# A hybrid recurrence and mixture-of-experts layer on one core: the first block's token list summed while experts are chosen

## The chip, the cores and the metric

The kernel runs on one core of a Trainium2 chip. The metric is the device time of one execution, in microseconds (us); lower is better.

## The reference, cut to what matters

One layer with 2048 tokens of 1024 channels: a mixer (a gated linear recurrence and a spatial gate behind one input projection, then one output projection with a residual), and then a mixture of experts with a residual, and a last RMSNorm. All is float32. The change touches the experts:

```
logits_g = h @ w_group + b_group          # 4 groups
logits_e = h @ w_router + b_router        # 32 experts, 8 in a group
g_sel    = argmax(logits_g)
top-2 of the 8 experts inside g_sel, weights = softmax
...
order    = argsort(expert)                # tokens sorted by expert,
padded   = ceil(counts / 128) * 128       # each expert's list filled up to blocks of 128
def expert_block(xb, e):                  # for each block
    return (silu(xb @ w_gate[e]) * (xb @ w_up[e])) @ w_down[e]
```

An expert's three matrices are 1024 x 512, 1024 x 512 and 512 x 1024: 2 MB each.

## The kernel before

The mixer fills the first 1120 us. Its last stage, `output_projection`, goes through 16 tiles of 128 tokens, from tile 15 down to tile 0. TensorE multiplies; VectorE adds the residual; a router's product gives the logits. `choose` takes the tiles in groups (12 to 15, 8 to 11, 4 to 7, 2 and 3, last 0 and 1): it finds each token's two experts as one-hot rows (`pick`), counts tokens by expert (`sums`), and gives each token its place in its expert's list: a block (`blk`) and a row in it, as a one-hot row of 128 (`at`). The tile's normalized rows `h` are stored to DRAM (`h_d`).

Then `routing`, a chain of small steps: counts of all tokens (`total`), blocks by expert (`ni`, `nb`), an order of experts (`key`, `ahead`), each expert's first block (`start`), and for four groups of four tiles a matrix `v`, whose product with `at` (64 matmul records on TensorE) sums up every block's token list. `index` is that table: column j has the 128 token numbers of block j.

`experts` works through the blocks. `load` brings an expert's matrices in six DMAs of 1 MB from SyncE's queue into `st` (two sets, for even and odd blocks). `high` and `low` split a staged matrix into two float32r parts (`wh` on ScalarE, `wl` on VectorE), so that a product is three matmuls of float32r: high by high, high by low, low by high. `fetch` is an indirect DMA of GpSimd's queue that gathers a block's 128 rows from `h_d` into `xg`. `turn_rows` transposes them on TensorE and splits them into `xh`, `xl`. `collect` weights the result and adds it to the rows of `acc_d`.

A scheduler sets the order of each engine's instructions, from a cost model and from priorities, except where `pin` keeps the order of the code. Each engine issues in its own order and waits there for what its next instruction needs; this holds for the DMAs that it issues too. Tiles come from pools of SBUF; a pool opened later takes the place of a closed one, and a tile in it waits until the last reader of what lay there is done. Here pool `lg` (logits and all of `routing`'s tables) is closed before pool `sp` opens at the same side. PSUM has eight banks in the first part; the tag `t2` is one of them, so a tile of `t2` waits for the reader of the one before.

Of the kernel before, what the change touches and what calls it, by code (L numbers as in the profile page):

```python
# [14 lines left out]
F32 = mybir.dt.float32  # L15
F32R = mybir.dt.float32r
# [9 lines left out]
P = 128  # L26
# [34 lines left out]
class Mixer:  # L61
# [617 lines left out]
    def output_projection(self, op, lg):  # L679
        nc, I = self.nc, self.I  # L680
        wh, wl = zip(*self.wo)
        with self.tc.tile_pool(name="os", bufs=2, reuse_waits="tile") as os_:
# [6 lines left out]
            def project(t, y, between, before):  # L689
# [29 lines left out]
                def normed(parts=(0, 1)):  # L719
                    for s in [fs[f] for f in parts]:  # L720
                        nc.vector.scalar_tensor_tensor(h[:, s], x[:, s], st[:, 2:3], rows["a2"][:, s], op0=ALU.mult, op1=ALU.mult)
                        nc.vector.tensor_add(h[:, s], h[:, s], rows["b2"][:, s])
                    if 1 in parts:

                        (nc.sync if t else nc.gpsimd).dma_start(self.h_d[t * P : (t + 1) * P], h)

                return x, st[:, 2:3], normed

# [50 lines left out]
            columns(done[0], done[1], 1)  # L779
            logits(0, *done[1:])  # L780
            chosen = self.choose(op, 0, 2, os_)
            with self.tc.issue_after(next(chosen)):
                normed((1,))
            next(chosen, None)
            self.routing(lg, os_)


    def routing_start(self, rt):
# [3 lines left out]
        def new(shape, name, dt=F32, **iota):  # L792
            x = rt.tile([P] + list(shape), dt, name=name)
            if iota:
                nc.gpsimd.iota(x, allow_small_or_imprecise_dtypes=True, **iota)
            return x
# [11 lines left out]
            "w": new([2, NT], "w"),  # L808
            "blk": new([2, NT], "blk"),
            "at": new([2, NT, P], "at"),  # L810
        }
        nc.gpsimd.memset(R["before"], 1.0)
        nc.gpsimd.affine_select(out=R["before"], in_=R["before"], compare_op=ALU.is_gt, fill=0.0, base=0, pattern=[[1, P]], channel_multiplier=-1)
        nc.vector.memset(R["sums"][:, NT], 0.0)
# [23 lines left out]
    def choose(self, L, t0, tn, tp):  # L838
# [5 lines left out]
        def new(shape, name, dt=F32):  # L844
            return tp.tile([P] + list(shape), dt, name=name, bufs=1)
# [47 lines left out]
        nc.vector.scalar_tensor_tensor(rw, R["blk"][:, :, ts], -float(P), place, op0=ALU.mult, op1=ALU.add)  # L893
        nc.vector.tensor_tensor(R["at"][:, :, ts], R["rows"].unsqueeze(1).unsqueeze(1).to_broadcast([P, 2, tn, P]), rw.unsqueeze(3).to_broadcast([P, 2, tn, P]), op=ALU.is_equal)

        e = new([tn, NG], "e")
        nc.vector.tensor_tensor(e, lg, bc(gm, [tn, NG], 2), op=ALU.subtract)
        nc.scalar.activation(e, e, AF.Exp)
# [6 lines left out]
        nc.vector.reciprocal(w1, den)  # L905
        nc.vector.tensor_mul(w2, w2, w1)

    def routing(self, rt, rv):


        nc, R, S = self.nc, self.R, self.tab
        new, row = R["new"], R["row"]

        total = self.psum("t1")
        nc.tensor.matmul(total[:, :NE], self.ones, R["sums"][:, 0], start=True, stop=True)
        nc.tensor.matmul(total[:, NE : NE + 1], R["sums"][:, : P // NE].rearrange("p t e -> p (t e)"), self.ones[:, :1], start=True, stop=True)
        ni = new([NE + 1], "ni", I32)
        nc.vector.tensor_scalar_add(ni, total[:, : NE + 1], float(P - 1))
        nc.vector.tensor_scalar(ni, ni, 7, None, op0=ALU.arith_shift_right)
# [61 lines left out]
    def experts(self, mp, sp, pp):  # L981
# [3 lines left out]

        xg = [mp.tile([P, D], F32, name=f"xg{n}") for n in range(2)]

        for x in xg:
            nc.gpsimd.memset(x, 0.0)
        acts = [mp.tile([P, 512], F32, name=f"a{n}") for n in range(2)]  # L990


        small = mp.tile([P, 96], F32, name="small")
        rows = [[sp.tile([P, KD, P], F32R, name=f"x{x}{n}") for x in "hl"] for n in range(2)]
        sp.tile([P, 64], F32, name="pad")
        parts = [[[sp.tile([P, 2, D], F32R, name=f"w{x}{s}{n}") for n in range(2)] for s in range(2)] for x in "hl"]
        g2 = self.row(sp, "g2")


        stage = [[[sp.tile([P, 2, D], F32, name=f"st{s}{part}{n}") for n in range(2)] for part in range(3)] for s in range(2)]  # L1000
# [51 lines left out]

        def fetch(j):
            if j <= MAXB:
                rows = bass.IndirectOffsetOnAxis(ap=S["index"][:, j : j + 1], axis=0)
                dma = nc.gpsimd.indirect_dma_start(xg[j % 2], None, self.h_d[:, :], rows, bounds_check=T - 1, oob_is_err=False)  # L1056
                self.got = dma.ins

# [40 lines left out]
        def sums():  # L1099
            return pp.tile([P, 2, 512], F32, name="sums", bufs=1)  # L1100

        def steps(js, end=None, whole=None):

            for j in js:
                a = acts[j % 2]
                if end is None:
                    fetch(j + 2)
                pg = bank()  # L1110
                product(j, 0, range(4), pg)
                if j:
                    high(j - 1, 2, 0)
                    high(j - 1, 2, 1)
                    low(j - 1, 2, 0, end)
                    act = turn_act(acts[(j - 1) % 2])
                    low(j - 1, 2, 1, end)
                if end is not None:
                    yield
                product(j, 0, range(4, KD), pg)  # L1120
                if j:
                    high(j, 1, 0)
                    low(j, 1, 0, end)
                    pin(nc.scalar.activation(a, pg, AF.Silu))
                high(j, 1, 1)
                low(j, 1, 1, end)
                if end is not None:
                    yield
                if not j:
                    pin(nc.scalar.activation(a, pg, AF.Silu))  # L1130
                    turn_rows(j + 1)
                else:
                    pd = sums()
                    down(j - 1, act, range(2), pd)
                    if end is None:
                        turn_rows(j + 1)
                    down(j - 1, act, range(2, 4), pd)
                    collect(j - 1, pd)
                    if j + 1 == end:
                        px = turn_rows(j + 1)  # L1140
                pu = bank()
                product(j, 1, range(KD), pu)
                if j != end:
                    high(j + 1, 0, 0)
                    low(j + 1, 0, 0, end)
                    high(j + 1, 0, 1)
                    if whole is not None:
                        pin(nc.scalar.activation(whole, px, AF.Copy))
                    pin(nc.vector.tensor_mul(a, a, pu))
                    low(j + 1, 0, 1, end)  # L1150
                else:
                    for n in range(2):
                        high(j, 2, n)
                        low(j, 2, n, end)
                    pin(nc.vector.tensor_mul(a, a, pu))
                if j + 1 == end:
                    yield
# [180 lines left out]

        for part in range(3):
            load(0, part)  # L1340
        place[0, 0] = 0
        for n in range(2):
            split(parts[0][0][n], parts[1][0][n], stage[0][0][n])
        fetch(0)
        high(0, 1, 0)
        low(0, 1, 0)
        turn_rows(0)
        for part in range(3):
            load(1, part)
        load(2, 0)  # L1350
        fetch(1)
        run(steps(range(MINB - 2)))
        with ExitStack() as behind:
            last = {i.engine: i for i in nc.cur_bb.bb.instructions}
            for engine in (SP, mybir.EngineType.PE, mybir.EngineType.Activation, mybir.EngineType.DVE, mybir.EngineType.Pool):
# [210 lines left out]
def layer(tc, ctx, I, out=None):  # L1566
# [26 lines left out]
    with tc.tile_pool(name="pp", bufs=1, space=PSUM) as pp:  # L1593
        M.pp = pp
        hp = ExitStack()
        with pool("ms", bufs=1) as ms:
# [6 lines left out]
        tab = ctx.enter_context(pool("tab", bufs=1))  # L1603
        M.tab = {
            "index": tab.tile([P, 64], I32, name="index"), "weight": tab.tile([P, 64], F32, name="weight"),
            "expert": tab.tile([1, NJ], I32, name="expert"), "fresh": tab.tile([1, NJ], I32, name="fresh"), "count": tab.tile([1, 16], I32, name="count")[:, :1],
        }
        with pool("lg", bufs=1, side="right") as lg:
            L = lg.tile([P, NT, NG + NE], F32, name="L")
            M.output_projection(L, lg)  # L1610
# [28 lines left out]
```

## Time and profile before

| | us |
|---|---|
| median of 3 runs | 2057.06 |
| lowest, highest | 2056.17, 2058.30 |
| the profiled execution, its own time | 2056.24 |
| its span, first to last instruction | 2054.5 |

A profile names instructions by line, engine, operation and tile. Busy time says how long an engine worked; the chain of waits says, followed back from the last instruction, which work or wait ended last at each moment. Times in the trace are counted from the span's start. The stretch that the change touches lies between 1120 and 1190 us: the end of the output projection, the routing, and the first block.

### The profile page before, as it was taken

How to read it: one execution, taken by the hardware profiler on the slowest of the kernel's cores; microseconds unless marked ns; L12 is line 12 of the kernel's file. 1: busy time of each engine (PE TensorE's matmuls, PEld its weight loads, DVE VectorE, ACT ScalarE, POOL GpSimd, SP SyncE). 2: the span in 40 equal slices, each digit the busy share in tenths (PEclk: the TensorE clock that was granted, in tenths of full speed). 3: DMA queues.
4: the chain of work that ended last, by engine and by line, in shares of the span. 5: the costliest groups of instructions: out<-in, count | busy, mean ns of one | idle time of the engine just before them, and what ended most of it. 6: DMA issues, size and time to landing. Idle time of an engine off the chain costs nothing.

```text
span 2054.5 us, 27982 instructions
## 1 busy us (share of the span) xinstructions
PE 1978.5 (96%) x9833; PEld 1630.2 (79%) x9833; DVE 1535.9 (75%) x2135; ACT 1113.1 (54%) x1265; POOL 310.1 (15%) x242
## 2 busy tenths in 40 slices
PE   7999999999999999989999599999999999999994
PEld 3787887888888888878888488888888888888881
DVE  6653337566666666646776799999999999999995
ACT  3664321334434344354542277777777777777773
POOL 1000001000000000110000122222222222232323
PEclk9999999999999999999999699999999999999997
DMA  7433749333333333486553888898887559888857
GB/s 277 148 116 102 249 149 320 125 104 104 119 105 116 101 104 114 156 273 223 187 197 118 326 298 262 295 349 291 275 302 251 169 190 336 282 295 256 307 174 312
DMA packets 224659, 435.46 MB, mean 212 GB/s; under 512 B 19799, under 2 KB 83859, under 8 KB 223730
## 3 DMA queue, kind: packets, MB, share of 16 engines
q1 hardware_dynamic: 206082, 384.83, 53.8%
q0 software_dynamic: 18416, 48.65, 8.6%
q8 instruction: 81, 1.33, 0.3%
q14 instruction: 80, 0.66, 0.1%
HBM read 460.28 MB, written 93.34 MB: 269 GB/s over the span
## 4 chain that ended last, share of the span: by engine, by line
PE 82%; DVE 8%; DMA 4%; ACT 2%; issue 1%; POOL 0%; another core or an unknown queue 0%; ACTq 0%; DVEq 0%; POOLq 0%; SPq 0%
PE bank L1084 25%; PE sums L1091 12%; PE ps_mm L80 8%; PE ps_mm L81 8%; PE ps_mm L79 8%; PE ps_mm L706 3%; PE ps_mm L708 3%; PE ps_mm L707 3%; PE turn_x L1064 2%; PE ps_t L738 1%; PE ps_t L1480 1%; PE turn_a L1064 1%; DMA out<-st 1%; PE ps_t L1504 1%; PE ps_t L1538 1%
## 5 line engine op out<-in xcount | busy, mean ns | idle before, releaser
L1045 DVE TENSOR_TENSOR wl<-st,wh 128x2048 fp32r<-128x2048 f32 x280 | 628.4, 2285 | 2.1 <-ACT wh L1038 1.4
L1038 ACT ACTIVATE wh<-st 128x2048 fp32r<-128x2048 f32 x280 | 533.9, 1916 | 70.8 <-PE bank L1084 61.6
L1084 PE MATMUL bank<-wh,xh 128*128 128x512 f32 x760 | 301.5, 397 | 1.1 <-ACT xh L1050 1.1
L1084 PE MATMUL bank<-wh,xl 128*128 128x512 f32 x760 | 297.2, 391 | 0.0
L1084 PE MATMUL bank<-wl,xh 128*128 128x512 f32 x760 | 296.5, 390 | 0.5 <-DVE wl L1045 0.5
L79 PE MATMUL ps_mm<-hTh,chi 128*128 128x512 f32 x632 | 249.6, 395 | 0.0
L80 PE MATMUL ps_mm<-hTl,chi 128*128 128x512 f32 x632 | 246.6, 390 | 0.0
L81 PE MATMUL ps_mm<-hTh,clo 128*128 128x512 f32 x632 | 246.4, 390 | 0.0
L1097 POOL DMA_INDIRECT acc_d<-y,index x46 | 154.4, 3357 | 228.5 <-DVE y L1095 225.3
L1084 PEld LDWEIGHTS bank<-wh,xl 128*128 128x128 f32 x760 | 143.0, 188 | 31.1 <-DVE xl L1051 0.8
L1084 PEld LDWEIGHTS bank<-wl,xh 128*128 128x128 f32 x760 | 143.4, 189 | 29.4 <-DVE wl L1045 1.1
L1084 PEld LDWEIGHTS bank<-wh,xh 128*128 128x128 f32 x760 | 143.3, 189 | 29.4 <-ACT xh L1050 1.5
L1091 PE MATMUL sums<-wh,ah 128*128 128x512 f32 x368 | 147.1, 400 | 0.0
L1091 PE MATMUL sums<-wh,al 128*128 128x512 f32 x368 | 143.6, 390 | 0.1
L1091 PE MATMUL sums<-wl,ah 128*128 128x512 f32 x368 | 143.5, 390 | 0.0
L79 PEld LDWEIGHTS ps_mm<-hTh,chi 128*128 128x128 f32 x632 | 118.8, 188 | 25.7 <-issue 1.7
L81 PEld LDWEIGHTS ps_mm<-hTh,clo 128*128 128x128 f32 x632 | 118.6, 188 | 24.7
L80 PEld LDWEIGHTS ps_mm<-hTl,chi 128*128 128x128 f32 x632 | 118.8, 188 | 24.4 <-issue 0.9
L1056 POOL DMA_INDIRECT xg<-h_d,index x48 | 70.6, 1472 | 374.9 <-PE turn_x L1064 358.3
L706 PE MATMUL ps_mm<-woh,yp 128*128 128x512 f32 x256 | 103.3, 404 | 1.3 <-ACT yp L70 1.3
L79 PE MATMUL ps_mm<-wnh,hTh 128*128 128x512 f32 x256 | 102.3, 400 | 0.3 <-ACT wnh L70 0.3
L708 PE MATMUL ps_mm<-woh,yp 128*128 128x512 f32 x256 | 100.8, 395 | 0.7 <-DVE yp L73 0.7
(404 smaller groups left out, 3449.0 us busy)
## 6 DMA issues: line engine op xcount, KB each, us to landing
st<-in_w_gate SPq DMA_DIRECT2D x98, 1024.0 KB
st<-in_w_up SPq DMA_DIRECT2D x96, 1024.0 KB
st<-in_w_down SPq DMA_DIRECT2D x96, 1024.0 KB
x<-in_x SPq DMA_DIRECT2D x32, 512.0 KB
wm<-in_w_mod SPq DMA_DIRECT2D x32, 512.0 KB
cst<-in_w_in SPq DMA_DIRECT2D x20, 512.0 KB
wst<-in_w_in SPq DMA_DIRECT2D x16, 512.0 KB
q<-q_d SPq DMA_DIRECT2D x32, 256.0 KB
```

Of the source, the lines that this page charges most:

```text
L79: nc.tensor.matmul(ps, sh(k), mh(k), start=k == 0, stop=False)
L80: nc.tensor.matmul(ps, sh(k), ml(k), start=False, stop=False)
L81: nc.tensor.matmul(ps, sl(k), mh(k), start=False, stop=k == nk - 1)
L706: nc.tensor.matmul(ps, yh[:, k], wh[k][:, s], start=k == 0, stop=False)
L708: nc.tensor.matmul(ps, yl[:, k], wh[k][:, s], start=False, stop=k == KD - 1)
L1038: pin(nc.scalar.activation(parts[0][at][n], stage[j % 2][part][n], AF.Copy))
L1045: pin(nc.vector.tensor_tensor(lo, stage[j % 2][part][n], hi.bitcast(F32), op=ALU.subtract))
L1056: dma = nc.gpsimd.indirect_dma_start(xg[j % 2], None, self.h_d[:, :], rows, bounds_check=T - 1, oob_is_err=False)
L1064: pin(nc.tensor.transpose(ps[:, k], x[:, k * P : (k + 1) * P], self.ident))
L1084: pin(nc.tensor.matmul(ps, m[:, k], w(k), start=k == n == 0, stop=k == KD - 1 and n == 2))
L1091: pin(nc.tensor.matmul(ps[:, f], m[:, k], w(k, f), start=k == n == 0, stop=k == 3 and n == 2))
L1097: nc.gpsimd.indirect_dma_start(self.acc_d[:, :], rows, y, None, bounds_check=T - 1, oob_is_err=False, compute_op=ALU.add)
```

## The change

While `choose` runs for a group of tiles, the token list of one block, the first (block 0 of expert 0), is added up as well: `mine` has the token number where a token's place is in expert 0's block 0, and `own` sums `at` times `mine` on VectorE; for the last group four small matmuls add the rest onto `own` in PSUM, in a tile of tag `t2`, and two VectorE steps make `first`, a column of 128 token numbers (tile `few`). The gather of block 0 uses `first` instead of `index`. The totals' two matmuls stand in front of the places' matmuls. Tile 0's store of `h` goes from ScalarE's queue, no longer from GpSimd's. One of the two zero fills of `xg` is written behind the first gather.

Block 0's gate and up are no longer split: they are plain float32 matmuls, 8 each, from the staged matrices and from a float32 transpose of the rows. In pool `sp` the tiles get other places: one set of split parts, `g2`, then the other set.

```diff
-                        (nc.sync if t else nc.gpsimd).dma_start(self.h_d[t * P : (t + 1) * P], h)
+                        (nc.sync if t else nc.scalar).dma_start(self.h_d[t * P : (t + 1) * P], h)
...
+        mine = new([2, tn], "mine")
+        nc.vector.scalar_tensor_tensor(mine, R["blk"][:, :, ts], 0.0, R["pick"][:, :, ts, 0], op0=ALU.is_equal, op1=ALU.mult)
+        nc.vector.tensor_tensor(mine, mine, R["tok"][:, ts].unsqueeze(1).to_broadcast([P, 2, tn]), op=ALU.mult)
+        places = [(s, n) for s in range(2) for n in range(tn)]
+        if t0:
+            for s, n in places:
+                nc.vector.scalar_tensor_tensor(R["own"], R["at"][:, s, t0 + n], mine[:, s, n : n + 1], R["own"], op0=ALU.mult, op1=ALU.add)
+        else:
+            ps = self.psum("t2")
+            nc.tensor.matmul(ps[:, :1], R["own"], self.ones[:, :1], start=True, stop=False)
+            for s, n in places:
+                nc.tensor.matmul(ps[:, :1], R["at"][:, s, n], mine[:, s, n : n + 1], start=False, stop=(s, n) == places[-1])
+            none = new([1], "none")
+            nc.vector.tensor_scalar(none, ps[:, :1], 0.0, float(T + 1), op0=ALU.is_equal, op1=ALU.mult)
+            nc.vector.scalar_tensor_tensor(self.tab["first"], none, -1.0, ps[:, :1], op0=ALU.add, op1=ALU.add)
...
-        for x in xg:
-            nc.gpsimd.memset(x, 0.0)
+        nc.gpsimd.memset(xg[0], 0.0)
...
-        parts = [[[sp.tile([P, 2, D], F32R, name=f"w{x}{s}{n}") for n in range(2)] for s in range(2)] for x in "hl"]
+        second = [[sp.tile([P, 2, D], F32R, name=f"w{x}1{n}") for n in range(2)] for x in "hl"]
         g2 = self.row(sp, "g2")
+        parts = [[[sp.tile([P, 2, D], F32R, name=f"w{x}0{n}") for n in range(2)], y] for x, y in zip("hl", second)]
...
-                rows = bass.IndirectOffsetOnAxis(ap=S["index"][:, j : j + 1], axis=0)
+                rows = bass.IndirectOffsetOnAxis(ap=S["index"][:, j : j + 1] if j else S["first"], axis=0)
...
-        place[0, 0] = 0
-        for n in range(2):
-            split(parts[0][0][n], parts[1][0][n], stage[0][0][n])
         fetch(0)
-        high(0, 1, 0)
-        low(0, 1, 0)
-        turn_rows(0)
-        for part in range(3):
+        nc.gpsimd.memset(xg[1], 0.0)
+        load(1, 0)
+        fetch(1)
+        for part in (1, 2):
             load(1, part)
-        load(2, 0)
-        fetch(1)
-        run(steps(range(MINB - 2)))
+        x = mp.tile([P, KD, P], F32, tag="y", name="y", bufs=1)
+        pin(nc.scalar.activation(x, turned(xg[0], "turn_x"), AF.Copy))
+        ps = [bank(), bank()]
+        for part in range(2):
+            for k in range(KD):
+                pin(nc.tensor.matmul(ps[part], x[:, k], stage[0][part][k // 4][:, k % 4 // 2, k % 2 * 512 : (k % 2 + 1) * 512], start=k == 0, stop=k == KD - 1))
+            load(2, part)
+            if part == 0:
+                fetch(2)
+                for n in range(2):
+                    high(1, 0, n)
+                    low(1, 0, n)
+                pin(nc.scalar.activation(acts[0], ps[0], AF.Silu))
+        pin(nc.vector.tensor_mul(acts[0], acts[0], ps[1]))
+        turn_rows(1)
+        run(steps(range(1, MINB - 2)))
```

How the instructions stand on three engines follows, each row with the counters that it waits for (`DMAHW` and `DMASW` count DMAs, the others an engine's instructions).

SyncE's queue at the end of the output projection, before. `row_g` is here the broadcast load of `g2`, and `st` are the staged matrices of block 0.

```order
L715 DMA acc_d<-x 128x1024 [waits DMAHW5_49,DVE_49]
L649 DMA row_g_9991<-g_d 128x1024 [waits DMASW2_49,DMASW1_49,DMASW3_49,DMASW0_49,PE_49]
L1018 DMA st_9993<-in_w_gate 128x4x512 [waits DMAHW3_49,DMASW6_49]
L1018 DMA st_9994<-in_w_gate 128x4x512
L1018 DMA st_9995<-in_w_up 128x4x512 [waits DMASW7_49,DMASW0_49]
L1018 DMA st_9996<-in_w_up 128x4x512 [waits DMAHW6_49]
```

The same place on SyncE's queue in the changed kernel.

```order
L715 DMA acc_d<-x 128x1024 [waits DMAHW5_49,DVE_49]
L649 DMA row_g_10040<-g_d 128x1024 [waits DMASW0_49,DVE_49,DMAHW3_49,PE_49,Pool_49]
L1045 DMA st_10046<-in_w_gate 128x4x512 [waits DMASW6_49,DMASW3_49]
L1045 DMA st_10047<-in_w_gate 128x4x512
L1045 DMA st_10048<-in_w_up 128x4x512 [waits DMASW7_49,DMAHW6_49,DMASW1_49,DMASW0_49]
L1045 DMA st_10049<-in_w_up 128x4x512 [waits DMAHW7_49]
```

The order is the same; the load of `g2` has new waits, for VectorE and GpSimd, and another count of TensorE. In the built program its tile lies at bytes 94080 to 98176 of a partition, where `lg` had the end of `at`, `own`, `start`, `late` and, last, `free`; its VectorE count is reached by the write of `index` (L1003) and its TensorE count by the last of the 32 list matmuls (L995). Before, the tile lay at byte 126848, where the low part of the output weights had been, and the wait was for their last matmul (L707).

GpSimd's queue from the zero fills of `xg` on, before (`xg_9971` and `xg_9972` are the two buffers).

```order
L725 DMA h_d<-h 128x1024 [waits DMASW6_49,DVE_49]
L989 MEMSET xg_9971 128x1024 [waits DMAHW5_49,DMAHW2_49]
L989 MEMSET xg_9972 128x1024 [waits DVE_49,PE_49,Activation_49]
L1056 DMA xg_9971<-h_d,index 128x1024 [waits DMAHW3_49,DMAHW2_49,DMAHW4_49,DMAHW0_49,DMAHW5_49,DMASW7_49,DMAHW6_49,DMASW6_49,DMAHW7_49,DVE_49,Pool_49]
L1056 DMA xg_9972<-h_d,index 128x1024 [waits DMASW0_49,Pool_49]
```

The same in the changed kernel, where `few` holds `first`.

```order
L88 TENSOR_TENSOR ost<-ms,nhalf 128x1 [waits DVE_49,Activation_49,Pool_49] x14
L1014 MEMSET xg_10025 128x1024 [waits DMAHW5_49,DMAHW2_49]
L1363 MEMSET xg_10026 128x1024 [waits DVE_49,PE_49,Activation_49]
L1083 DMA xg_10025<-h_d,few 128x1024 [waits DMAHW3_49,DMAHW4_49,DMAHW2_49,DMAHW6_49,DMAHW0_49,DMAHW7_49,DMASW6_49,Pool_49]
L1083 DMA xg_10026<-h_d,index 128x1024 [waits DMASW7_49,DVE_49,Pool_49]
```

The store of `h` is gone from this queue; the second zero fill still stands ahead of the first gather, as before. In both kernels that fill waits for the third of the four groups of list matmuls, since its buffer lies where a `v` was.

TensorE from the last places to the lists, in the changed kernel.

```order
L910 MATMUL ps_t_9875<-ones,own 128x1 [waits DVE_49]
L933 MATMUL ps_t_9852<-sums,ones 128x32 [waits DVE_49]
L934 MATMUL ps_t_9852<-ones,sums 128x1
L886 MATMUL ps_t_9858<-oh,before 128x64 [waits PE_49]
L887 MATMUL ps_t_9858<-sums,ones 128x64
L912 MATMUL ps_t_9875<-mine,at 128x1 [waits DVE_49]
L912 MATMUL ps_t_9875<-mine,at 128x1 x3
L954 MATMUL ps_t_9904<-ahead,ones 128x32 [waits DVE_49]
L973 MATMUL ps_t_9925<-ident,be 1x128 [waits DVE_49,PE_49]
```

Before, the matmul of `ahead` came right behind the totals; now the four of L912 stand between, and `ps_t_9904` and `ps_t_9875` are both the one bank of tag `t2`, so `ahead`'s matmul waits for the step that writes `first` (L915).

## Rows read from the trace of the kernel before

**Rows 1.** The page: busy time, share of the span and instructions of each engine.

```profile
PE 1978.5 (96%) x9833; PEld 1630.2 (79%) x9833; DVE 1535.9 (75%) x2135; ACT 1113.1 (54%) x1265; POOL 310.1 (15%) x242
```

**Rows 2.** The chain of waits in order of time, 1120 to 1190 us: start, us, what.

```profile
1136.66 1.50 DVE ni L919
...
1139.48 0.20 DVE ahead L926
...
1140.40 0.19 DVE start L941
...
1154.70 2.07 PE ps_t L969 x16
...
1157.05 0.23 DVE index L977
...
1158.13 5.67 DMA xg<-h_d,index
...
1163.85 1.98 PE turn_x L1064 x8
...
1182.13 2.79 PE bank L1084 x11
```

**Rows 3.** The timeline of SyncE's queue, 1119 to 1185 us: start, us, what.

```profile
1126.08 0.32 SPq L649 DMA_DIRECT2D row_g<-g_d  x1
1126.49 1.36 SPq L1018 DMA_DIRECT2D st<-in_w_gate  x2
...
1146.12 18.07 SPq L1018 DMA_DIRECT2D st<-in_w_up  x2
1164.98 0.95 SPq L1018 DMA_DIRECT2D st<-in_w_down  x2
```

**Rows 4.** Who waited for whom, SyncE's queue, 1120 to 1200 us: total us, times, longest.

```profile
SPq L1018 <- DMA xg<-h_d,index: 17.1, 1, 17.1
```

**Rows 5.** The view of stretches: us, busy time of each engine, granted clock, DMA share, GB/s.

```profile
1126.50:1132.00 5.50, 1.74 (x8) 1.60 (x8) 3.82 (x18) 0.67 (x2) 0.55 (x1) 0.57 1.00 249
1132.00:1155.50 23.50, 11.88 (x66) 10.99 (x67) 20.72 (x78) 3.61 (x3) 2.51 (x3) 0.59 1.04 397
...
1168.00:1210.00 42.00, 41.47 (x191) 34.01 (x191) 32.73 (x21) 29.40 (x22) 7.87 (x4) 0.96 1.03 378
```

**Rows 6.** The timeline of VectorE, 1119 to 1185 us.

```profile
1122.15 0.17 DVE L890 TENSOR_SCALAR pi<-pi 128x4 int32<-128x4 int32 x1
...
1122.56 0.16 DVE L893 SCALAR_TENSOR_TENSOR rw<-blk,place 128x4 f32<-128x4 f32 x1
...
1124.13 0.69 DVE L709 TENSOR_TENSOR h<-ps_mm,row_g 128x512 f32<-128x512 f32 x1 [0.69 <-PE ps_mm L708]
...
1134.19 0.42 DVE L878 TENSOR_TENSOR sums<-sums,oh 128x32 f32<-128x32 f32 x2
...
1136.59 1.57 DVE L919 TENSOR_SCALAR ni<-ni 128x33 int32<-128x33 int32 x1
...
1177.98 1.22 DVE L1051 TENSOR_TENSOR xl<-turn_x,xh 128x1024 fp32r<-128x1024 f32 x1 [6.98 <-ACT xh L1050]
```

**Rows 7.** The timeline of GpSimd, 1119 to 1185 us.

```profile
1136.56 0.60 POOL L725 DMA_DIRECT2D h_d<-h  x1 [9.15 <-DVE ni L918]
1137.15 0.97 POOL L989 MEMSET xg<- 128x1024 f32 x1
1154.54 0.95 POOL L989 MEMSET xg<- 128x1024 f32 x1 [16.42 <-PE ps_t L969]
```

**Rows 8.** The instructions of line 1509: a float32 step of VectorE that multiplies 128 x 128 by a column and adds 128 x 128; shortest, median and longest in ns.

```profile
L1509 DVE SCALAR_TENSOR_TENSOR state<-state,both,ps_t x120: 319/346/351, 402.0 to 890.0; 128x128 f32<-128x128 f32 x120
```

**Rows 9.** The timeline of TensorE, at three places; a plain float32 matmul is two records, a float32r matmul one.

```profile
1135.52 0.56 PE L916 MATMUL ps_t<-ones,sums 128*128 128x1 f32 x2
...
1182.47 0.39 PE L1084 MATMUL bank<-wh,xl 128*128 128x512 f32 x1
...
2001.86 7.03 PE L1267 MATMUL bank<-st,st 128*128 128x512 f32 x16
```

**Rows 10.** The page's costliest groups, two of them: count, busy us, mean ns of one, idle time before.

```profile
L1045 DVE TENSOR_TENSOR wl<-st,wh 128x2048 fp32r<-128x2048 f32 x280 | 628.4, 2285 | 2.1 <-ACT wh L1038 1.4
L1038 ACT ACTIVATE wh<-st 128x2048 fp32r<-128x2048 f32 x280 | 533.9, 1916 | 70.8 <-PE bank L1084 61.6
```

**Rows 11.** The timeline of ScalarE, 1119 to 1185 us.

```profile
1175.14 1.28 ACT L1130 ACT_TABLE_LOAD   x1 [6.46 <-PE bank L1084]
1176.43 0.60 ACT L1130 ACTIVATE a<-bank 128x512 f32<-128x512 f32 x1
1176.93 1.02 ACT L1050 ACTIVATE xh<-turn_x 128x1024 fp32r<-128x1024 f32 x1
```

**Rows 12.** The view of stretches, half a microsecond each; the granted clock is the third number from the end.

```profile
1161.00:1161.50 0.50, 0.00 (x0) 0.00 (x0) 0.50 (x1) 0.00 (x0) 0.50 (x1) 0.86 0.73 98
...
1171.50:1172.00 0.50, 0.50 (x4) 0.42 (x3) 0.00 (x0) 0.00 (x0) 0.00 (x0) 0.90 1.03 401
```

**Rows 13.** The instructions that write or read `xg`, 1120 to 1200 us: time of its gathers from issue to landing.

```profile
DMA to landing us min/median/max: 5.2/7.0/9.5
```

**Rows 14.** What TensorE waited for from 830 to 1125 us, the first and the last of four rows: total us, times, longest.

```profile
PE ps_t L1538 <- DVE o L1545: 3.2, 1, 3.2
...
PE ps_mm L708 <- DVE yp L73: 0.7, 1, 0.7
```

More of the change, by code (lines that the diff above doesn't have):

```diff
@@ L781, in output_projection @@
             chosen = self.choose(op, 0, 2, os_)
-            with self.tc.issue_after(next(chosen)):
+            behind = next(chosen)
+            total = self.totals()
+            with self.tc.issue_after(behind):
                 normed((1,))
             next(chosen, None)
-            self.routing(lg, os_)
+            self.routing(lg, os_, total)
     def routing_start(self, rt):
@@ L810, in routing_start @@
             "at": new([2, NT, P], "at"),
+            "own": new([P], "own"),
         }
+        nc.gpsimd.memset(R["own"], 0.0)
         nc.gpsimd.memset(R["before"], 1.0)
@@ L906, in choose, with totals @@
         nc.vector.tensor_mul(w2, w2, w1)
-    def routing(self, rt, rv):
-        nc, R, S = self.nc, self.R, self.tab
-        new, row = R["new"], R["row"]
+    def totals(self):
+        nc, R = self.nc, self.R
         total = self.psum("t1")
@@ L916, in routing @@
         nc.tensor.matmul(total[:, NE : NE + 1], R["sums"][:, : P // NE].rearrange("p t e -> p (t e)"), self.ones[:, :1], start=True, stop=True)
+        return total
+    def routing(self, rt, rv, total):
+        nc, R, S = self.nc, self.R, self.tab
+        new, row = R["new"], R["row"]
         ni = new([NE + 1], "ni", I32)
@@ L1111, in steps @@
                 product(j, 0, range(4), pg)
[L1112 to L1117, printed above, removed]
+                high(j - 1, 2, 0)
+                high(j - 1, 2, 1)
+                low(j - 1, 2, 0, end)
+                act = turn_act(acts[(j - 1) % 2])
+                low(j - 1, 2, 1, end)
                 if end is not None:
@@ L1120, in steps @@
                 product(j, 0, range(4, KD), pg)
[L1121 to L1124, printed above, removed]
+                high(j, 1, 0)
+                low(j, 1, 0, end)
+                pin(nc.scalar.activation(a, pg, AF.Silu))
                 high(j, 1, 1)
@@ L1128, in steps @@
                     yield
-                if not j:
-                    pin(nc.scalar.activation(a, pg, AF.Silu))
+                pd = sums()
+                down(j - 1, act, range(2), pd)
+                if end is None:
                     turn_rows(j + 1)
[L1132 to L1140, printed above, removed]
+                down(j - 1, act, range(2, 4), pd)
+                collect(j - 1, pd)
+                if j + 1 == end:
+                    px = turn_rows(j + 1)
                 pu = bank()
@@ L1605, in layer @@
             "index": tab.tile([P, 64], I32, name="index"), "weight": tab.tile([P, 64], F32, name="weight"),
-            "expert": tab.tile([1, NJ], I32, name="expert"), "fresh": tab.tile([1, NJ], I32, name="fresh"), "count": tab.tile([1, 16], I32, name="count")[:, :1],
+            "expert": tab.tile([1, NJ], I32, name="expert"), "fresh": tab.tile([1, NJ], I32, name="fresh"),
         }
+        few = tab.tile([P, 16], I32, name="few")
+        M.tab.update(count=few[:1, :1], first=few[:, 1:2])
         with pool("lg", bufs=1, side="right") as lg:
```

## The prediction

> **What bounds the kernel now.** I read the page first: TensorE is busy for 96% of the span [rows 1], so what the change can win lies where TensorE stands. Then the chain of waits between 1120 and 1190 us, which shows that place: from the choice of the last two tiles to block 1 the end is carried by VectorE's small steps, then the list matmuls, the gather, and only then TensorE again [rows 2]. Third, the timelines of SyncE, VectorE, GpSimd and ScalarE in that stretch [rows 3, 6, 7, 11], to see what is done beside the chain. What the reader is to see there: the weights of block 0 are issued at 1126.49, before the routing begins [rows 3], and the DMA engines are full with them from 1126.5 to 1155.5 (share 1.00 to 1.04 [rows 5]). The routing hides some 10 MB of loads. I take as the mark the third product of block 1's gate, at 1182.47 [rows 9]: from there TensorE runs without a wait worth naming until the end phase, and what that point slips, the end slips.
>
> **1. The chain to the experts' first blocks** (`start`, 1140.40 before [rows 2]). Sums ready at 1134.19 + 0.42 = 1134.61 [rows 6].
>
> - *The list of block 0 in the earlier groups:* 8 + 8 + 8 + 4 steps of VectorE on 128 x 128. The nearest row is a step of that form: 0.346 us [rows 8]; 28 of them are 9.7 us. They lie under the output projection, where TensorE waits 6.5 us in all in 295 us, in no case for line 709 or 710 [rows 14]. I take nothing for the first 24. The last 4 and two `mine` steps stand around the last additions of tile 0, which the chain needs. Two steps of 0.16 plus about 0.03 between [rows 6] and two of 0.35 are 1.08, of which the 0.69 that VectorE idles before line 709 [rows 6] hides the most; a third one stands between lines 709 and 710: 0.39 + 0.35 = 0.7 us late. Bounds: 0 (all hidden) to 1.8 (none).
> - *The shift `ni`* takes 1.57 us [rows 6], a shift of the same kind 0.17 [rows 6]. Its end, 1138.16, is that of GpSimd's store issue and zero fill (1136.56 to 1138.12 [rows 7]). With the store on ScalarE and the zero fill free to run earlier, 1.4 us go. The Trainium skill, page "SBUF — State Buffer", section "Who interferes with whom", says that VectorE in some forms and GpSimd take one pair of ports in turn, and the later one is blocked for the whole instruction; the rows agree, and by the rule too the gain is these 1.4 us. Were the shift slow by itself, they would not come back. I take 1.4, and 0.2 from the totals that go ahead of the places: `ahead` is ready 3.5 after the sums instead of 1139.68 - 1134.61 = 5.1.
> - *The wait that is new:* `ahead`'s matmul must now wait for `first`, since both use the one bank of `t2`. Between stand the row in the block, `mine`, `at`, `mine` (1.05 us in the now alternating order), four matmuls (L916's record pair took 0.56 in all; issued 0.4 apart that is 1.75 [rows 9]) and two steps (0.35): `ahead`'s matmul starts 3.2 us after its input instead of at once, and `start` stands 7.4 after the sums instead of 5.8.
>
> Sum: 0.7 + 1.6 = 2.3 us later, `start` at 1142.7. Bounds 1.0 to 4.5.
>
> **2. The gather of block 0.** In the order of GpSimd's queue the second zero fill stands ahead of it, and that fill waits for the third group of list matmuls; before, it ran at 1154.54 [rows 7], 14.1 after `start`. The order of VectorE now interleaves the first two `v`, so the first group starts 0.9 later and the lists end 0.9 later. So: 1142.7 + 14.1 + 0.9 + 0.95 (the fill) + 0.4 = 1159.1 instead of 1158.13. The rows land 5.67 [rows 2] to 7.0 us [rows 13] later: 1164.8 to 1166.1 (1163.80 before). "At once" is therefore not what the queue does.
>
> **3. The weights.** SyncE issues in its order: before, the second half of block 1's up waits 17.1 us for a gather, and the downs behind it wait too [rows 3, 4]. Now the load of `g2`, which stands ahead of all weights, waits for the write of `index`. That is at 1142.7 + 17.8 = 1160.5 (1157.28 - 1140.40 = 16.9 after `start` before [rows 2], plus 0.9). So the loads of block 0 begin at 1160.5 and not at 1126.5: 34 us of full DMA engines are lost as cover.
>
> Block 1's gate is needed split, as before. Until its second half has landed there pass: `g2` 0.5 MB, two to three gathers 1.0 to 1.6, and eight loads of 1.05 MB, 9.9 to 10.5 MB. The same queue began before with 249 GB/s for 5.5 us (1.4 MB) and then ran at 397 [rows 5]: 5.5 + 8.5 to 9.1 MB at 397 = 26.9 to 28.4 us; at 397 from the start 25.0 to 26.4; at 378, the rate among running blocks [rows 5], 26.2 to 27.8. Bounds 1185.5 to 1188.9; I take 1187.5, which is near the repeat of that beginning.
>
> **4. From there to the mark.** ScalarE's order after that landing: the high part 1.92 [rows 10], the table load 1.28 and 0.50 until the next one starts, `xh` 1.02 [rows 11]: 1192.2. VectorE: the low part 2.29 behind the high one [rows 10], `a` 0.69, `xl` 1.22 [rows 6]: 1187.5 + 1.92 + 2.29 + 0.69 + 1.22 = 1193.6 with the gaps at most 1193.8. The mark moves from 1182.47 to 1193.6: +11.1.
>
> *What lies beside it:* the plain gate and up. Eight plain matmuls took 7.03 us at full clock [rows 9], 0.86 each after the first; 16 are 13.8. From 1169 (rows landed, 1.98 for the transposes [rows 2], 1.02 for the copy) with 2.3 lost at half clock they end at about 1185, before the split gate is there. They cost nothing here; the cover that hides them is the wait for weights. If that cover goes, see rival B.
>
> *The clock.* After the last list matmul (1154.70 + 2.07 = 1156.77 [rows 2]) TensorE stood, and the granted clock fell from 1.00 (2.4 GHz) to 0.50 (1.2 GHz) at about 1161.4 [rows 12], 4.6 us on. Dense work began at 1166.9 (1163.85 + 1.98 and the split's 1.02 [rows 2, 11]), and the clock rose at about 1171.6 [rows 12]. In the changed kernel TensorE stands from 1186 to 1192, longer than those 4.6 us, so I expect the low clock again, and 4.7 us of dense work at half speed cost 2.3 us. Bounds 0 and 2.6.
>
> **Sum.** 11.1 + 2.3 = 13.4 us, with the bounds of DMA, chain and clock 9 to 16. Everything behind the mark moves as a whole. Against the profiled execution: 2056.24 (span 2054.5 and 1.7 around it) + 13.4 = 2069.6; it lies 0.8 under the median of 2057.06, so I predict 2070.5 as a median, and 2066 to 2073 if the steps hold.
>
> **Rivals.**
>
> *A. The weights stay late.* From then on a block needs up to 6.3 MB of weights, 0.5 of gather and 0.5 of scattered rows (1.0 if adding reads them too): 7.3 to 7.8 MB in the 17.7 us that a block takes, 412 to 441 GB/s against 378 to 397 [rows 5]. Before, 30 us of head start covered this. If the first blocks all bring a new expert, each slips by 0.7 to 2 us until one comes that needs no load; over four to six blocks 3 to 10 us more: 2073 to 2081. Against it: before, the queue was full from 1168 to 1210 and then had room, and stages are loaded two blocks ahead.
>
> *B. SyncE's queue isn't held* (the counter is reached earlier than I read it). Then the rows decide: landed at 1164.8, transposes 1.98, copy 1.1, 13.8 + 2.3, `turn_rows` of block 1 0.9 and its `xh` 1.1 and `xl` 1.3, which nothing hides now: the mark at 1187.3, +4.8; with the clock kept 1183.9, +1.4. 2058.5 to 2061.9. It decides if the gates of block 0 are issued near 1126 again.
>
> *C. It does what its words say, and isn't slower.* If the gather went out while the lists are still summed and the weights were there, TensorE could go from the lists (ended at 1159.8) straight on at full clock: 1.0 + 1.1 + 13.8 + 0.9 + 1.1 + 1.3 = 19.2, the mark at 1179.0, 3.5 us ahead: 2053.6. For it speaks the size of the hole (1156.77 to 1163.85 [rows 2]); against it the orders of two queues. It decides if the first gather is issued before the second zero fill.
>
> **How the numbers follow.** Forecast 0.75, A 0.12, B 0.09, C 0.04. The range of 2061 to 2078 takes in the forecast's own, most of A and the upper end of B. A measurement of this kernel can't tell less than 0.2% (4.1 us) from no change: C and two thirds of B fall within it. Faster 0.02, the same 0.08, slower 0.90.
>
> **What would show it.** In the profile of the changed kernel: the load of `g2` and the first gate loads issued behind the write of `index`, near 1160, with DMA share near 0 from 1128 on and near 1 from 1161 to beyond 1210; the second zero fill right ahead of the first gather; `ni` at about 0.2 us; `ahead`'s matmul behind L915; ScalarE waiting for `st` of block 1, and TensorE standing some 6 us behind the plain up, at the low clock after that. I am wrong if the gates are issued at 1126, if block 1's gate lands before 1182, or if TensorE waits for weights again in blocks 2 to 5.

## The result and the profile after

The changed kernel takes 2071.22 us (median of 4 runs, 2070.38 to 2071.71) against 2056.61 us for the kernel before, measured beside it: a ratio of 1.0073, 95% interval 1.006 to 1.0086. It is slower by 14.6 us, as forecast. The profiled execution took 2071.48, with a span of 2069.7.

TensorE is busy 9 us longer [rows 1]. That sum mixes new work (the plain products, the list's small matmuls) with work at the low clock, and the waits come on top, so it tells little here.

```profile
PE 1987.4 (96%) x9827; PEld 1630.8 (79%) x9827; DVE 1532.6 (74%) x2170; ACT 1105.7 (53%) x1261; POOL 308.1 (15%) x242
```

The timeline of SyncE's queue answers to [rows 3]: start, us, what. Nothing is issued between 1127.5 and 1160.4, and the first weights follow at 1160.80.

```profile
1127.17 0.32 SPq L715 DMA_DIRECT2D acc_d<-x  x1
1160.39 0.32 SPq L649 DMA_DIRECT2D row_g<-g_d  x1
1160.80 0.94 SPq L1045 DMA_DIRECT2D st<-in_w_gate  x2
1161.90 3.93 SPq L1045 DMA_DIRECT2D st<-in_w_up  x2
```

Who waited on that queue, 1120 to 1200 us (total, times, longest), answers to [rows 4]. The load of `g2` waits for `index`; the 17.1 us for a gather are gone.

```profile
SPq L649 <- DVE index L1003: 32.8, 1, 32.8
```

The stretches beside [rows 5]; the last three numbers are the granted clock, the DMA share and GB/s. The DMA engines are idle while experts are chosen, and full after that.

```profile
1132.00:1155.50 23.50, 10.06 (x51) 9.17 (x51) 19.25 (x86) 0.20 (x1) 0.00 (x0) 0.56 0.06 23
1155.50:1160.50 5.00, 4.10 (x32) 3.72 (x32) 2.64 (x7) 0.00 (x0) 2.09 (x2) 1.00 0.00 0
1160.50:1166.00 5.50, 1.97 (x8) 1.57 (x8) 0.00 (x0) 0.62 (x1) 1.44 (x2) 0.74 0.78 237
1166.00:1189.00 23.00, 16.90 (x40) 7.73 (x40) 0.00 (x0) 2.31 (x2) 1.54 (x2) 0.84 1.05 398
```

GpSimd's timeline, beside [rows 7]: the second zero fill waits 27.9 us for the lists, and the gather with `first` (`few`) stands right behind it.

```profile
1157.79 0.95 POOL L1363 MEMSET xg<- 128x1024 f32 x1 [27.90 <-PE ps_t L995]
1158.96 1.14 POOL L1083 DMA_INDIRECT xg<-h_d,few  x1 [0.21 <-POOL xg L1363]
```

VectorE's timeline, beside [rows 6]: the last sums, the shift `ni`, `start` and `index`. The shift takes 0.17 us instead of 1.57.

```profile
1135.63 0.42 DVE L882 TENSOR_TENSOR sums<-sums,oh 128x32 f32<-128x32 f32 x2
...
1138.31 0.17 DVE L945 TENSOR_SCALAR ni<-ni 128x33 int32<-128x33 int32 x1
...
1143.55 0.19 DVE L967 COPY start<-ps_t 128x32 f32<-128x32 f32 x1 [0.67 <-PE ps_t L954]
...
1160.03 0.22 DVE L1003 SCALAR_TENSOR_TENSOR index<-free,ps_t 128x64 int32<-128x64 f32 x1
```

TensorE's timeline from the first list matmuls to the mark, the third product of block 1's gate (line 1111, `wh,xl`). Behind the lists three waits stand ahead of it: for the gather, for the first gate, and 8.37 us for `xh`.

```profile
1149.96 5.22 PE L995 MATMUL ps_t<-v,at 128*128 128x128 f32 x32 [4.39 <-DVE v L992]
...
1163.33 1.97 PE L1091 MATMUL turn_x<-ident,xg 128*128 128x128 f32 x8 [3.59 <-DMA xg<-h_d,few]
1169.23 16.02 PE L1375 MATMUL bank<-st,y 128*128 128x512 f32 x32 [3.93 <-DMA st<-in_w_gate]
...
1194.49 0.80 PE L1111 MATMUL bank<-wh,xh 128*128 128x512 f32 x1 [8.37 <-ACT xh L1077]
...
1195.75 0.79 PE L1111 MATMUL bank<-wh,xl 128*128 128x512 f32 x1
```

That wait names ScalarE, but ScalarE was late itself, as its timeline shows: it waits for the gate of block 1, whose second half is there at 1189.71, and the split, the table load, `silu` and `xh` follow one another.

```profile
1189.71 1.91 ACT L1065 ACTIVATE wh<-st 128x2048 fp32r<-128x2048 f32 x1 [0.72 <-DMA st<-in_w_gate]
1191.63 1.28 ACT L1382 ACT_TABLE_LOAD   x1
1192.93 0.60 ACT L1382 ACTIVATE a<-bank 128x512 f32<-128x512 f32 x1
1193.42 1.02 ACT L1077 ACTIVATE xh<-turn_x 128x1024 fp32r<-128x1024 f32 x1
```

The mixer before this stretch ends up to 4 us apart between these profiles, also between two of the same kernel (run 5 below has its last sums at 1131.86 and 1134.74). So I compare marks by their distance from the row of the last sums: before 1182.47 - 1134.19 = 48.28 [rows 6, 9], after 1195.75 - 1135.63 = 60.12. The stretch is 11.8 us longer. Each row below has one profile per kernel, and the last column is its distance less 48.28.

### The profile page after: what moved, and what is told of

Same layout as the page of the kernel before. It is cut to its first block, busy times and chain, and to the rows that moved or that the text cites. A ratio compares the mean times of both kernels' runs of the same rounds, so it can differ in the third digit from the quotient of the medians.

```text
span 2069.7 us, 27987 instructions
## 1 busy us (share of the span) xinstructions
PE 1987.4 (96%) x9827; PEld 1630.8 (79%) x9827; DVE 1532.6 (74%) x2170; ACT 1105.7 (53%) x1261; POOL 308.1 (15%) x242
## 4 chain that ended last, share of the span: by engine, by line
PE 82%; DVE 8%; DMA 5%; ACT 2%; issue 1%; SPq 1%; POOL 0%; another core or an unknown queue 0%; ACTq 0%; DVEq 0%; POOLq 0%
PE bank L1111 25%; PE sums L1118 12%; PE ps_mm L80 8%; PE ps_mm L81 8%; PE ps_mm L79 8%; PE ps_mm L706 3%; PE ps_mm L708 3%; PE ps_mm L707 3%; PE turn_x L1091 2%; PE ps_t L738 1%; PE ps_t L1513 1%; PE turn_a L1091 1%; DMA out<-st 1%; DMA wst<-in_w_in 1%; PE ps_t L1571 1%
## 5 line engine op out<-in xcount | busy, mean ns | idle before, releaser
L1111 PE MATMUL bank<-wh,xh 128*128 128x512 f32 x744 | 295.2, 397 | 8.4 <-ACT xh L1077 8.4
L1111 PE MATMUL bank<-wh,xl 128*128 128x512 f32 x744 | 291.2, 391 | 0.0
L1111 PE MATMUL bank<-wl,xh 128*128 128x512 f32 x744 | 290.4, 390 | 0.0
L1083 POOL DMA_INDIRECT xg<-h_d,index x47 | 66.2, 1409 | 390.3 <-PE turn_x L1091 388.2
```

Source lines behind the costliest of these rows:

```text
L1111: pin(nc.tensor.matmul(ps, m[:, k], w(k), start=k == n == 0, stop=k == KD - 1 and n == 2))
```

## The experiments

| kernel | median, us | ratio to before, 95% | last sums, us | mark, us | mark after sums | against before |
|---|---|---|---|---|---|---|
| changed kernel | 2071.22 | 1.0073 (1.006 to 1.0086) | 1135.63 | 1195.75 | 60.12 | +11.8 |
| `g2` last | 2058.37 | 1.0005 (0.9995 to 1.0014) | 1135.93 | 1185.68 | 49.75 | +1.5 |
| `g2` on ScalarE | 2057.71 | 1.0002 (0.9992 to 1.0012) | 1134.10 | 1183.25 | 49.15 | +0.9 |
| gather first | 2068.72 | 1.0055 (1.0038 to 1.0072) | 1134.88 | 1193.96 | 59.08 | +10.8 |
| both | 2052.32 | 0.9973 (0.9964 to 0.9983) | 1133.63 | 1178.29 | 44.66 | -3.6 |
| both, list in `t0` | 2051.15 | 0.9971 (0.996 to 0.9983) | 1131.86 | 1174.37 | 42.51 | -5.8 |
| the same once more | 2050.94 | 0.9974 (0.9963 to 0.9985) | 1134.74 | 1177.30 | 42.56 | -5.7 |
| before, tiles only | 2069.13 | 1.0056 (1.004 to 1.0072) | 1135.01 | 1194.20 | 59.19 | +10.9 |
| split again | 2055.86 | 0.9991 (0.9982 to 1.0) | 1134.48 | 1180.71 | 46.23 | -2.1 |
| store on GpSimd | 2052.19 | 0.9978 (0.9969 to 0.9988) | 1133.16 | 1177.71 | 44.55 | -3.7 |
| rows early | 2048.18 | 0.9958 (0.9942 to 0.9975) | 1134.12 | 1174.95 | 40.83 | -7.5 |

**1. `g2` last in its pool.**

```diff
-        g2 = self.row(sp, "g2")
         parts = [[[... name=f"w{x}0{n}") ...
+        g2 = self.row(sp, "g2")
```

> The changed kernel with one thing undone: g2's tile comes last in its pool again, so that its load no longer waits for a tile of the routing. If SyncE's held queue is the cause, the gates of block 0 are issued near 1127 again, the gather (still behind the second zero fill) decides, and the third product of block 1's gate slips by 1 to 5 us against the kernel before, not 13: 2057 to 2061. If the new steps themselves (the float32 products, the wait for the first list, the late gather) are the cause, the time stays at 2067 to 2072.

2058.37 us: 12.9 of the 14.6 us are back with one line moved. SyncE's queue and TensorE in this run:

```profile
1128.35 1.30 SPq L1045 DMA_DIRECT2D st<-in_w_gate  x2
```

```profile
1163.49 1.97 PE L1091 MATMUL turn_x<-ident,xg 128*128 128x128 f32 x8 [3.48 <-DMA xg<-h_d,few]
1166.62 15.76 PE L1375 MATMUL bank<-st,y 128*128 128x512 f32 x32 [1.16 <-ACT y L1371]
...
1185.68 0.50 PE L1111 MATMUL bank<-wh,xl 128*128 128x512 f32 x1 [0.53 <-DVE xl L1078]
```

The gates are issued at 1128.35, and TensorE waits for the late gather, then for no weight. With the gather still late, all the new steps together neither cost nor win anything that can be measured.

**2. `g2` loaded from ScalarE's queue**, each tile where the change put it.

```diff
-        g2 = self.row(sp, "g2")
+        g2 = self.row(sp, "g2", self.nc.scalar)
```

The diff is cut here: `row` takes the queue as a new argument.

> The changed kernel, every tile where it is, but g2's load goes from ScalarE's queue. The load waits for the same write of the index as before, only the weights no longer stand behind it. If it is the order of the queue that costs (and not the tile's place as such), the weights go out near 1127 and the time is that of the run with g2's tile last, 2057 to 2061. If the weights' tiles themselves wait for the routing, the time stays at 2071.

2057.71 us. The load still waits for `index` (ScalarE's queue), but the weights no longer stand behind it (SyncE's queue):

```profile
1159.72 0.33 ACTq L649 DMA_DIRECT2D row_g<-g_d  x1
```

```profile
1126.57 1.25 SPq L1045 DMA_DIRECT2D st<-in_w_gate  x2
```

So it is the order of the queue that costs; a load that starts 33 us late costs nothing where nobody is behind it.

**3. The gather first.** Only the second zero fill is held back: `issue_after` puts it behind the gather on GpSimd.

```diff
         fetch(0)
-        nc.gpsimd.memset(xg[1], 0.0)
+        with tc.issue_after(self.got):
+            nc.gpsimd.memset(xg[1], 0.0)
```

> The changed kernel with one thing added: the second zero fill is held behind the first gather, so that block 0's rows are gathered while the lists are summed, and SyncE's queue is held as it was. If the weights set the end, the rows come some 10 us sooner and the time stays at 2071, within 1.5. If the late gather was the cause, some 4 us come back: 2067.

2068.72 us, 2.5 under the changed kernel and between the two answers (the intervals of the two ratios overlap). The gather went out at 1142.94, and TensorE's wait for rows became one for weights:

```profile
PE bank L1376 <- DMA st<-in_w_gate: 8.3, 1, 8.3
```

So the early rows by themselves gain nothing: TensorE stands for the weights instead. What came back lies elsewhere. At the mark it is 1.0 us: from the first gate's issue to the second split of block 1's gate there are now 27.9 us (1160.01 to 1187.91) instead of 28.9. That fits the half megabyte of block 0's rows, which no longer shares the DMA engines there (1.3 us at 398 GB/s). Behind the mark it is the clock: after the last wait TensorE ran at the low clock for 3.7 us here and 6.2 in the changed kernel, which makes 1.1 us up to the first product of block 0's down (line 1118). I had priced neither, so the band of 1.5 us was too narrow; that the weights bind is borne out.

**4. Both edits.** 

> Both edits together: g2's tile last and the second zero fill behind the first gather. If the change does what its words say once the two queues let it, TensorE goes from the lists straight on to the float32 products at full clock, and the time is 2051.5 to 2054 (3 to 5 us under the kernel before). If the low clock comes all the same, or the rows of block 1 decide, 2055 to 2058.

2052.32 us, 3.5 to 7.4 us under the kernel before by the interval. TensorE goes from the lists to block 0 with one wait of 1.16 us, and the granted clock stays at 1.00 (2.4 GHz) where it was 0.50 (1.2 GHz) with `g2` last alone. TensorE, then the stretch here, then a stretch of the run with `g2` last:

```profile
1156.90 2.05 PE L995 MATMUL ps_t<-v,at 128*128 128x128 f32 x16 [0.45 <-DVE v L992]
1158.79 1.04 PE L1091 MATMUL turn_x<-ident,xg 128*128 128x128 f32 x8
1160.98 14.00 PE L1376 MATMUL bank<-st,y 128*128 128x512 f32 x32 [1.16 <-ACT y L1372]
```

```profile
1160.00:1165.00 5.00, 4.02 (x10) 1.87 (x11) 2.24 (x2) 4.53 (x3) 2.01 (x2) 1.00 0.44 125
```

```profile
1165.00:1170.00 5.00, 3.84 (x7) 1.56 (x6) 1.60 (x1) 4.46 (x3) 0.99 (x1) 0.50 0.64 197
```

What one edit is worth hangs on the other: the early gather brings 2.5 us while the weights are late and 6 once they are not, and `g2` last brings 12.9 with the late gather and 16.4 with the early one.

**5. The list in another PSUM bank**, with both edits.

```diff
-            ps = self.psum("t2")
+            ps = self.psum("t0")
```

> Both edits (g2's tile last, second zero fill behind the first gather) and the first block's list in PSUM bank t0 instead of t2, so that the matmul of ahead no longer waits for it. If that wait was worth what I put it at, start comes about 1.7 us sooner than with both edits alone, and so do the lists and the end: 2050 to 2052. If the chain has room there, no difference from the run with both edits.

2051.15 and, on another chip, 2050.94 us (where 2050 to 2052 was expected again). TensorE now takes `ahead` first, and VectorE's steps behind `start` wait for the list instead. TensorE, then VectorE:

```profile
1135.93 0.63 PE L954 MATMUL ps_t<-ahead,ones 32*128 32x32 f32 x2 [1.63 <-DVE ahead L952]
```

```profile
1138.71 0.16 DVE L914 TENSOR_SCALAR none<-ps_t 128x1 f32<-128x1 f32 x1 [1.71 <-PE ps_t L912]
```

From the last sums `start` comes 3.0 us sooner than in run 4 (1136.74 - 1131.86 = 4.88 against 1141.55 - 1133.63 = 7.92), but the list matmuls only 1.0 sooner (13.35 against 14.34), since line 914 stands ahead of the steps that they need. So the wait that I put at 1.7 is worth 1.0 at the lists. In the whole time the two kernels can't be told apart: the ratios are 0.9973, 0.9971 and 0.9974. The other 1.1 of the marks' 2.1 is the clock of the lists, last section.

**6. The kernel before with the new order of tiles alone.**

```diff
-        parts = [[[... name=f"w{x}{s}{n}") for n in range(2)] for s in range(2)] for x in "hl"]
+        second = [[... name=f"w{x}1{n}") for n in range(2)] for x in "hl"]
         g2 = self.row(sp, "g2")
+        parts = [[[... name=f"w{x}0{n}") for n in range(2)], y] for x, y in zip("hl", second)]
```

> The kernel before with the changed kernel's order of tiles alone, nothing of its computation. g2's load then waits for a tile of the routing here too, and the weights of block 0 go out some 34 us later. If the held queue is the cause by itself, the time is 2062 to 2068, and the first wait for weights is that of block 0's split. If only the new steps with it make the loss, 2056.6.

2069.13 us, 1.1 above the expected band. The kernel before took 2057.76 beside it, so another order of tiles makes 11.4 of the 14.6 us, with nothing of the new computation; at the mark it is 10.9 of 11.8. SyncE's queue, and what TensorE waited for at 1160 to 1180 us:

```profile
1158.68 0.32 SPq L649 DMA_DIRECT2D row_g<-g_d  x1
```

```profile
PE turn_x L1065 <- DMA xg<-h_d,index: 9.6, 1, 9.6
PE bank L1085 <- ACT xh L1051: 7.4, 1, 7.4
```

I had looked for the first wait at the split's weights. TensorE's first wait is for the gather (issued 1159.39, there at 1167.6, 8.2 us instead of 5.7 [rows 2]), which now shares the DMA engines with the late weights: their share is 0.95 while it runs, before 0.27. The split comes second: `xh` stands behind it on ScalarE, which waits 2.0 us for the gate and 1.5 for the up.

**7. Block 0's split back**, on top of the list in `t0` and both edits: gate and up as in the kernel before, on the early rows. The diff is cut: the loop over blocks does block 0 again, and the loads and gathers behind it stand in their old order.

```diff
+        for n in range(2):
+            split(parts[0][0][n], parts[1][0][n], stage[0][0][n])
         fetch(0)
...
-        x = mp.tile([P, KD, P], F32, tag="y", name="y", bufs=1)
-        pin(nc.scalar.activation(x, turned(xg[0], "turn_x"), AF.Copy))
...
+        high(0, 1, 0)
+        low(0, 1, 0)
+        turn_rows(0)
```

> As the run with the list in bank t0, g2's tile last and the gather first, but block 0's gate and up are split into float32r parts as before. This parts the early list and gather from the plain float32 products. If the plain products cost (16 of 0.86 us against 24 float32r ones and a split that the routing hides), this is 1 to 3 us faster than that run; if they pay, since no split stands ahead of them, it is 1 to 3 us slower.

2055.86 us: 4.7 slower than without the split (3.7 at the mark), above the expected 1 to 3. The expectation's 24 float32r products are those of the gate alone; with the up they are 48. VectorE, then TensorE:

```profile
1158.77 4.49 DVE L1076 TENSOR_TENSOR wl<-st,wh 128x2048 fp32r<-128x2048 f32 x2
...
1165.38 1.22 DVE L1076 TENSOR_TENSOR xl<-turn_x,xh 128x1024 fp32r<-128x1024 f32 x1
```

```profile
1166.65 0.79 PE L1109 MATMUL bank<-wh,xl 128*128 128x512 f32 x1 [4.86 <-DVE xl L1076]
```

The three `wl` come behind `index` on VectorE, and `xl` behind them. In the kernel before they lay beside the gather, which hid them. With the rows early the split is bare, and the plain products pay because they need none. Whether the split would cost as much with `xl` ahead of the last `wl` on VectorE is open; no run has that order.

**8. Tile 0's store back on GpSimd**, otherwise as run 5.

```diff
-                        (nc.sync if t else nc.scalar).dma_start(...)
+                        (nc.sync if t else nc.gpsimd).dma_start(...)
```

> The run with the list in bank t0, g2's tile last and the gather first, with tile 0's store of h back on GpSimd's queue, where the zero fill stands behind it. If the store issue and the fill are what held the shift ni for 1.57 us in the kernel before, a VectorE step of 0.2 us takes 1.3 to 1.7 us again beside them, start comes 1.4 us later, and the end with it: 1 to 1.5 us slower than that run. If the shift was slow by itself, nothing changes.

2052.19 against 2050.94 us of run 5's kernel measured beside it: 1.25 slower, though the intervals of the two ratios overlap. GpSimd, then VectorE:

```profile
1135.77 0.60 POOL L725 DMA_DIRECT2D h_d<-h  x1 [9.58 <-DVE h L722]
1136.36 0.97 POOL L1014 MEMSET xg<- 128x1024 f32 x1
```

```profile
1135.84 1.53 DVE L945 TENSOR_SCALAR ni<-ni 128x33 int32<-128x33 int32 x1
```

The shift is held until the fill ends: 1.53 us instead of 0.18 in run 5. From the last sums `start` comes 1.26 us later than in the second profile of run 5 (6.13 against 4.87), and the lists 1.20 later, which is the size of the difference in time. The other 0.8 of the marks' 2.0 is the clock of the lists (10.7 us against 9.9, last section).

**9. Block 1's rows early**, on top of run 5.

```diff
                 pin(nc.tensor.matmul(ps[part], x[:, k], ..., start=k == 0, stop=k == KD - 1))
+                if (part, k) == (1, 3):
+                    turn_rows(1)
...
-        turn_rows(1)
```

> The run with the list in bank t0, g2's tile last and the gather first, with block 1's row transposes moved in between the float32 products, behind the fourth of block 0's up. xh and xl of block 1 are then made while TensorE multiplies. If the 1.2 and 0.5 us that TensorE waits for them between the blocks are all that they cost, 1.5 to 2 us come back: 2049 to 2050. If the rows land too late for the earlier place, or VectorE's order puts xl behind a split, nothing comes back.

2048.18 us, the best here: 8.6 us under the kernel before (ratio 0.9958) and 23 under the changed one. TensorE goes on without a wait:

```profile
1171.05 3.60 PE L1376 MATMUL bank<-st,y 128*128 128x512 f32 x8
1174.09 0.80 PE L1111 MATMUL bank<-wh,xh 128*128 128x512 f32 x1
```

The mark comes 1.7 us sooner than in run 5, as priced. The median moved by 2.8; in the two profiles the span behind the last sums is 1.5 us shorter, so the rest is not behind the mark, and no run here separates it from the spread of the mixer.

## Why the prediction was right

The time (2071.22 against 2070.5) and the cause were as forecast; single terms were not, and their errors nearly cancel: that the total came within 0.7 us is partly luck.

- *The held queue.* Forecast: weights from 1160.5, DMA share near 0 until then. Measured: 1160.80, and 0.06 and 0.00. The time agrees so well because this profile's mixer ends 1.4 us later: counted from the last sums it is 25.2 us where I had 26.3. Runs 1 and 2 take the hold away in two ways and get nearly all back; run 6 adds it alone and makes most of the loss. Shown from both sides.
- *The chain to `start`.* From the last sums to `start` it took 1143.55 - 1135.63 = 7.92 us, before 1140.40 - 1134.19 = 6.21: +1.7 where I said 2.3, of it 1.6 behind the sums. The term that failed is the 0.7 for `own` between lines 709 and 710: from line 709 to the last sums it took 10.06 before [rows 6] and 10.04 after (1125.59 to 1135.63), so all of it was hidden. The new wait took 3.24 us (`ahead` ready at 1139.64, its matmul at 1142.88) where I said 3.2. The shift's 1.4 came as forecast, and run 8 shows by itself that GpSimd's two instructions held it. By the Trainium skill, page "SBUF — State Buffer", section "Who interferes with whom", VectorE in a two-port mode and GpSimd lock each other out, and the later one is blocked for the whole instruction of the other. The trace agrees that the shift is held; it was held over two instructions in a row, 1.53 us in run 8.
- *`start` to `index`.* I added 0.9 for the interleaved `v`; measured 16.5 us from start to start (1160.03 - 1143.55) against 16.65 before. In the sum nothing of it came, though not for want of the cause: the first list matmul starts 6.41 us behind `start` (1149.96) instead of 5.82 (1146.22, below), so 0.6 of the 0.9 is there. The lists then took 9.78 us instead of 10.53, since the clock rose sooner in them, and that hid it. This is luck (last section).
- *The landing of block 1's gate.* Forecast 27.0 us after the queue's start, bounds 25.0 to 28.4; measured 28.9 (1160.80 to 1189.71), outside them. This term was mis-sized by 1.9: the queue began as I took it (237 GB/s for 5.5 us), but 10.7 MB had passed by then (5.5 us at 237 GB/s and 23.7 at 398) where I counted 9.9 to 10.5, and 27.0 goes with the lower end. Three gathers were out by 1166 and a fourth at 1186.4, where I took two to three; one gather less makes 1.0 us in run 3. A small term was put at nothing: 0.55 us lie between the end of `index`'s write (1160.25) and the first gate's issue. With this, and less the two terms above that did not come, the mark is at +11.8 instead of +11.1.
- *The gather* landed 4.4 us after its issue (1158.96 to 1163.33), where I took 5.67 to 7.0. The difference lies on GpSimd: it took 1.14 us to issue the gather and before 2.50 (below). Beside the 2.50 VectorE split weights, as beside the 2.51 of run 7's first gather by `index`; beside the 1.14 it had only the small steps of `index`. It did not matter here, since the first gate came later. GpSimd, before:

```profile
1158.13 2.50 POOL L1056 DMA_INDIRECT xg<-h_d,index  x1 [2.64 <-DMA st<-in_w_up]
```

- *The plain products cost nothing*, forecast to end near 1185 and hidden by the wait for weights: they ended at 1185.25 (1169.23 + 16.02). Run 7 then shows their worth without that cover: they win 4.7 us.
- *The clock.* Forecast: low again after the second standing, 2.3 us. The rows of two short stretches after: while TensorE stands, it falls at about 1190.4, and it rises at about 1200.7.

```profile
1190.00:1191.00 1.00, 0.00 (x0) 0.00 (x0) 1.00 (x1) 1.00 (x1) 0.00 (x0) 0.72 1.08 399
1200.00:1201.00 1.00, 1.00 (x6) 0.81 (x5) 0.00 (x0) 0.00 (x0) 0.00 (x0) 0.66 1.00 377
```

  From the mark to that rise the products start 0.43 apart instead of 0.23. TensorE, before (the first list matmuls and the first product of block 0's down), then the same product after:

```profile
1146.22 8.21 PE L969 MATMUL ps_t<-v,at 128*128 128x128 f32 x48 [3.20 <-DVE v L966]
...
1187.97 0.39 PE L1091 MATMUL sums<-wh,ah 128*128 128x512 f32 x1
```

```profile
1203.63 0.39 PE L1118 MATMUL sums<-wh,ah 128*128 128x512 f32 x1
```

  It starts 7.88 us behind the mark (1203.63 - 1195.75) instead of 5.50 (1187.97 - 1182.47): 2.4, as forecast. Mark and clock are 14.2; the span, less its shift at the sums, grew by 15.2 - 1.4 = 13.8, so the end phase gives some 0.4 back.
- *The rivals.* A (weights stay late) did not come: behind the mark TensorE waits for no weight. B's case is run 1, with the gates issued near 1128: 2058.37 against 2058.5 to 2061.9, just under its lower end. Its working was not right in all: the products began at the low clock (0.50, the second stretch shown under run 4), for which B had the mark at +4.8, and it came at +1.5. The rows were there 19.6 us behind `start` (1143.85 to 1163.49) where B had 22.1. C, once the two queues let it, is run 4: 2052.32 against 2053.6. Its working held: from the end of the lists to the mark it took 19.3 us (1158.95 to 1178.29) where C had 19.2. For the change as made C did not come, as forecast.

## What to carry to other kernels

A tile's place in a pool is part of the order of a queue: a small load with no hurry, put over the tables that were read last, held the weights back for 34 us because it stood at their head. After a change of tiles, read what the first load behind each pool waits for, and who stands behind it. A transfer goes out early only if its own queue lets it, so the zero fill behind the gather is as much a part of the change as the early list.

## What was not expected of the hardware

The low clock lasts for different times at the same place. When the list matmuls begin, the granted clock is 0.50 (1.2 GHz); it rose to 1.00 (2.4 GHz) 6.0 us later in run 4 and 3.0 later in run 5, and the same 64 records' lists took 11.0 and 9.8 us. TensorE and a stretch of run 4, then of run 5:

```profile
1147.97 8.48 PE L995 MATMUL ps_t<-v,at 128*128 128x128 f32 x48 [4.39 <-DVE v L992]
```

```profile
1147.50:1154.00 6.50, 6.03 (x28) 6.03 (x29) 5.46 (x16) 0.00 (x0) 0.00 (x0) 0.50 1.04 388
```

```profile
1145.21 5.26 PE L995 MATMUL ps_t<-v,at 128*128 128x128 f32 x32 [4.45 <-DVE v L992]
```

```profile
1148.00:1149.00 1.00, 1.00 (x10) 1.00 (x10) 0.49 (x4) 0.00 (x0) 0.00 (x0) 0.88 1.05 393
```

So 1.2 us of the mark's distance can be this alone, and a difference of that size between two single profiles says little of an edit; the medians decide.
